# Squares' additions and low parts of weights on GpSimd at the end of the first layer

## The chip, the cores and the metric

The kernel runs on one core of a Trainium2 chip. The metric is the device time of one execution in microseconds (us), the median of three runs; lower is better. The core has five engines with queues of their own: PE (TensorE, matmuls), DVE (VectorE), ACT (ScalarE), POOL (GpSimd) and SP (SyncE, which here issues most weight loads). They run side by side and wait for each other by semaphores. Each works through its own list of instructions in a fixed order, so one instruction that waits holds up all that stand behind it on that engine.

## The reference, cut to what matters

A network of two layers over 1024 latent tokens and 256 context tokens, 1024 features wide. Layer 0 mixes tokens with a convolution module, layer 1 with attention (16 query heads, 4 key and value heads, all of 64 features). Each layer ends with a SwiGLU feed-forward network. Each part is normed before and after it:

```python
hx = rmsnorm(x, norm_g[i, 0]) * (1.0 + sc_x) + sh_x
yx = conv_module(hx, ...)             # layer 0; layer 1: attention_module
x = x + g_x * rmsnorm(yx, norm_g[i, 1])
fx = rmsnorm(x, norm_g[i, 2]) * (1.0 + scf_x) + shf_x
x = x + gf_x * rmsnorm(swiglu(fx, ffn_w1[i], ffn_w3[i], ffn_w2[i]), norm_g[i, 3])
```

```python
def attention_module(hx, hc, wq, wk, wv, wo, q_g, k_g, cos, sin, need_ctx):
    qx = apply_rope(rmsnorm((hx @ wq).reshape(B, S, N_HEADS, HEAD_DIM), q_g), cos, sin)
    kx = apply_rope(rmsnorm((hx @ wk).reshape(B, S, N_KV_HEADS, HEAD_DIM), k_g), cos, sin)
    vx = (hx @ wv).reshape(B, S, N_KV_HEADS, HEAD_DIM)
    ...
```

`rmsnorm` needs the sum over all features of the squares of a token's values.

## The kernel before

Features lie on the 128 partitions, tokens along the free axis; a tile of 1024 features is eight pieces of 128 features, k or d from 0 to 7. The tokens are the context, the left 512 and the right 512 latent tokens (below "left" and "right").

A float32 product is made of three faster ones. Each operand is split into a high part, rounded, and a low part, what is left; high times high, low times high and high times low are added in one PSUM bank. For a weight piece `wload` does the split: SP loads the raw piece (L143), ACT casts it to the high part (`wh`, L144), and a subtraction makes the low part (`wl`): L148 on DVE or L150 on POOL. The counter `share` chooses between them: it grows by `lo_dve` with every piece, and at 1 the subtraction goes to DVE. `lo_dve` is 1 for nearly all of the kernel before, so that all subtractions are on DVE. There are three buffers for raw pieces here (`wr` twice, `q` once), and three each for the high and low parts.

The end of the first layer is a place where three things overlap:

- The feed-forward network of the right tokens ends. Its last product is evicted from PSUM, d by d, by an addition on DVE (`evict`, L926), and behind each eviction `sq_acc` squares the piece on ACT (L390, into one of four buffers `sb`) and adds the square to the row sums `acc` (L391). PE then sums over the partitions (L365).
- The left tokens, finished earlier, are normed for the attention: `apply`, for each k, multiplies (DVE, L399, into one of the same four `sb`), makes the high part (ACT, L404) and the low part (DVE, L405) of the input to the attention.
- The projections of the left tokens start: keys (PE L183 to L185, in two banks for the even and odd features), values (L172 to L174 with the weight as the first operand, 256 columns), and the eight pieces of the query weights (L172 to L174).

Then the norm of the right tokens' output is applied (`final`: L693 and L696 on DVE, results stored by POOL's L1374), its squares are added (L391 again), and the right tokens are projected in the same way. `qk_pair` norms and rotates keys and queries: squares on ACT (L1007, L1008), sums on PE (L1015), products with cosine and sine on DVE (L1033 to L1036), the split (ACT L1040, DVE L1042). POOL issues the loads of cosine and sine (L1052, L1053), the stores of keys and queries (L1056, L1080) and the loads of what was stored (L1095, L1102). The first matmul of the attention is L1116, and `attention` sets `lo_dve` to 1 itself.

The order on each engine is not written out. Pieces of work are generators (`pump` runs the background queue `bgq` next to the main one by estimated times), and a scheduler below them orders the instructions of each engine by its own estimates of their durations. A change of engine therefore also reorders others.

Of the kernel before, what the change touches and what calls it, by code (L numbers as in the profile page):

```python
# [12 lines left out]
ALU = mybir.AluOpType  # L13
# [42 lines left out]
class Kern:  # L56
# [323 lines left out]
                                    self.c["ident"][:w, :w])  # L380
        return pb[:, :n]

    def sq_acc(self, acc, src, k):
        nc = self.nc
        n = src.shape[-1]
        if k == 0:
            nc.scalar.activation(acc, src, AF.Square)
            return
        sq = self.sb(n)
        nc.scalar.activation(sq, src, AF.Square)  # L390
        nc.vector.tensor_tensor(acc, acc, sq, op=ALU.add)  # L391

    def apply(self, src, pb, l, i, segs, hi, lo, k, full=None):

# [404 lines left out]
    def ffn(self, l, fs, ytags, htags, boxes, tanh=False, parts=1, tail=None, fast=None):  # L799
# [3 lines left out]
        nc = self.nc  # L803
# [142 lines left out]
        def last(ds, j, c0, c1, ws, sums):  # L946

            fts = GROUPS[-1]
            G = len(fts)
            outs = [self.bank("mm") for _ in ds]  # L950
            self.mm3s(outs, [lambda k, d=d: ws[d * G + k] for d in ds],
                      lambda k: [v[:, c0:c1] for v in slot[fts[k]][j]], G, c1 - c0)
            for d, out in zip(ds, outs):
                evict(len(GROUPS) - 1, out, j, d, c0, c1, sums)
# [15 lines left out]
        for j, n in enumerate(ns):  # L970
            for part in range(parts):
                c0, c1 = part * n // parts, (part + 1) * n // parts
                if tail is None:
                    yacc = yaccs[j] if len(ns) > 1 else self.acc(n)
                    sums = lambda yd, d: self.sq_acc(yacc, yd, d)
                else:
                    sums = tail[part]

                m = 4 if parts > 1 and part == 0 else 2 if j == 0 and part == 0 else 1
                d = 0  # L980
                while d < KT:
                    last(range(d, d + m), j, c0, c1, ws, sums)
                    yield 3 * G * m * (c1 - c0) / 2400
                    d += m
                    m = 1
                if tail is None:
                    boxes[j].append((ys[j], yacc))
                else:
                    boxes[j].append(ys[j][:, :, c0:c1])
# [201 lines left out]
    def build(self):  # L1191
        nc, a, c = self.nc, self.a, None
# [216 lines left out]
        self.drain()  # L1409
        self.root = True  # L1410
        hs = self.T("HS", [P, 4, 512])
        self.bgq.append(self.qkv(hL[0], CTX, 512, self.wk, hs[:, :2], (hs[:, 2:],)))
        self.pump(7)
        self.kub = self.T("KB", [P, 2 * TOK], F32R)
# [309 lines left out]
```

## Time and profile before

| | |
|---|---|
| median of 3 runs | 2939.29 us (2937.05 to 2940.01) |
| the profiled execution | 2938.98 us, of which the span from the first to the last instruction is 2937.2 us |
| granted PE clock, mean | 0.987 |
| busy share of the span | PE 97%, DVE 74%, ACT 45%, POOL 8% |
| key projection of the left tokens on PE | 1440.98 to 1463.34 us |
| first matmul of the attention | 1573 us |

The profile is of one execution. Times of rows count from the start of the span. A row of a timeline has the start, the duration, the engine, the line, the operation and its operands by the program's names, and in brackets the idle time of the engine before it and what ended that. Where a row stands for several instructions in a row (x2), the duration is that of all. A row of the windows has, behind the stretch and its length, the busy time and count of PE, the weight loads, DVE, ACT and POOL, then the granted PE clock, the share of the DMA engines and GB/s.

### The profile page before, as it was taken

How to read it: one execution, taken by the hardware profiler on the slowest of the kernel's cores; microseconds unless marked ns; L12 is line 12 of the kernel's file. 1: busy time of each engine (PE TensorE's matmuls, PEld its weight loads, DVE VectorE, ACT ScalarE, POOL GpSimd, SP SyncE). 2: the span in 40 equal slices, each digit the busy share in tenths (PEclk: the TensorE clock that was granted, in tenths of full speed). 3: DMA queues.
4: the chain of work that ended last, by engine and by line, in shares of the span. 5: the costliest groups of instructions: out<-in, count | busy, mean ns of one | idle time of the engine just before them, and what ended most of it. 6: DMA issues, size and time to landing. Idle time of an engine off the chain costs nothing.

```text
span 2937.2 us, 42731 instructions
## 1 busy us (share of the span) xinstructions
PE 2847.7 (97%) x16462; PEld 2446.1 (83%) x16462; DVE 2160.7 (74%) x3746; ACT 1335.5 (45%) x2229; POOL 222.6 (8%) x377
## 2 busy tenths in 40 slices
PE   7999989999999999999999999989999999999998
PEld 6888877888888889989888787767777778889997
DVE  6887788847556378877786899786666666786777
ACT  5222255532222245544445688645555543444444
POOL 0000001011022001000011111110000000010000
PEclk9999999999999999999999999999999999999999
DMA  6443444334356224333345211322222143353332
GB/s 249 140 120 98 116 131 145 135 116 143 115 175 198 65 74 165 114 104 112 109 156 170 88 46 46 97 87 81 66 73 83 60 149 99 110 170 104 102 98 75
DMA packets 131755, 336.58 MB, mean 115 GB/s; under 512 B 31328, under 2 KB 52864, under 8 KB 130656
## 3 DMA queue, kind: packets, MB, share of 16 engines
q1 hardware_dynamic: 78016, 222.33, 24.1%
q0 software_dynamic: 29344, 103.83, 10.7%
q10 hardware_dynamic: 24192, 7.70, 1.1%
q8 instruction: 129, 2.11, 0.3%
q14 instruction: 74, 0.61, 0.1%
HBM read 289.50 MB, written 38.93 MB: 112 GB/s over the span
## 4 chain that ended last, share of the span: by engine, by line
PE 86%; DVE 7%; ACT 2%; issue 2%; DMA 2%; ACTq 0%; POOL 0%; SPq 0%; DVEq 0%; POOLq 0%
PE ps L172 15%; PE ps L173 15%; PE ps L174 15%; PE ps L875 4%; PE ps L877 4%; PE ps L876 4%; PE ps L1116 4%; PE ps L1134 4%; PE ps L1140 2%; PE ps L454 2%; PE ps L455 2%; PE ps L456 2%; PE ps L1141 2%; PE ps L185 1%; PE ps L183 1%
## 5 line engine op out<-in xcount | busy, mean ns | idle before, releaser
L172 PE MATMUL ps<-T,wh 128*128 128x512 f32 (+1 forms) x1360 | 502.5, 370 | 1.4 <-ACT T L161 0.8
L174 PE MATMUL ps<-T,wl 128*128 128x512 f32 (+1 forms) x1360 | 500.4, 368 | 2.0 <-DVE wl L148 2.0
L173 PE MATMUL ps<-T,wh 128*128 128x512 f32 (+1 forms) x1312 | 481.4, 367 | 0.2 <-DVE T L164 0.2
L144 ACT CAST wh<-wr 128x1024 fp32r<-128x1024 f32 (+1 forms) x217 | 225.0, 1037 | 419.9 <-PE ps L173 307.2
L148 DVE TENSOR_TENSOR wl<-wr,wh 128x1024 fp32r<-128x1024 f32 (+1 forms) x217 | 261.9, 1207 | 168.5 <-ACT wh L144 167.1
L875 PE MATMUL ps<-T,wh 128*128 128x256 f32 x1092 | 310.7, 285 | 5.0 <-ACT wh L161 4.5
L876 PE MATMUL ps<-T,wh 128*128 128x256 f32 x1092 | 306.5, 281 | 0.0
L877 PE MATMUL ps<-T,wl 128*128 128x256 f32 x1092 | 305.4, 281 | 0.2 <-DVE wl L164 0.2
L1138 DVE TENSOR_TENSOR T<-ps,T 128x512 fp32r<-128x512 f32 x320 | 216.8, 687 | 107.6 <-ACT T L1137 106.8
L172 PEld LDWEIGHTS ps<-T,wh 128*128 128x128 f32 x1360 | 257.8, 190 | 43.7 <-ACT T L1506 1.7
L174 PEld LDWEIGHTS ps<-T,wl 128*128 128x128 f32 x1360 | 257.7, 190 | 42.4 <-DVE wl L148 2.2
L173 PEld LDWEIGHTS ps<-T,wh 128*128 128x128 f32 x1312 | 248.5, 189 | 38.2 <-DVE T L164 1.3
L1137 ACT CAST T<-ps 128x512 fp32r<-128x512 f32 x320 | 186.0, 586 | 191.1 <-PE ps L1134 177.6
L173 PE MATMUL ps<-HS,wh 128*128 128x512 f32 x656 | 257.9, 393 | 0.0
L172 PE MATMUL ps<-HS,wh 128*128 128x512 f32 x608 | 238.4, 392 | 0.9 <-ACT wh L144 0.9
L174 PE MATMUL ps<-HS,wl 128*128 128x512 f32 x608 | 237.5, 391 | 0.0
L875 PEld LDWEIGHTS ps<-T,wh 128*128 128x128 f32 x1092 | 206.1, 189 | 11.2 <-ACT wh L161 6.7
L876 PEld LDWEIGHTS ps<-T,wh 128*128 128x128 f32 x1092 | 206.6, 189 | 0.5
L877 PEld LDWEIGHTS ps<-T,wl 128*128 128x128 f32 x1092 | 206.2, 189 | 0.6 <-DVE wl L164 0.4
L1134 PE MATMUL ps<-cst,T 128*128 128x128 f32 x1100 | 189.6, 275 | 3.2 <-DVE T L1138 3.1
L1122 DVE TENSOR_SCALAR_CACHE_REDUCE T<-ps,rq 128x1280 f32<-128x1280 f32 x110 | 170.0, 1546 | 27.9 <-PE ps L1116 22.1
L1134 PEld LDWEIGHTS ps<-cst,T 128*128 128x128 f32 x1100 | 132.6, 141 | 49.5 <-DVE T L1138 30.8
(377 smaller groups left out, 6195.9 us busy)
## 6 DMA issues: line engine op xcount, KB each, us to landing
wr<-in_w SPq DMA_DIRECT2D x170, 512.0 KB, 3.6
wr<-in_pw SPq DMA_DIRECT2D x35, 512.0 KB, 3.5
HV<-in_wmodT POOLq DMA_DIRECT2D x56, 256.0 KB, 4.1
q<-in_wmodT POOLq DMA_DIRECT2D x56, 256.0 KB, 3.9
KB<-in_w SPq DMA_DIRECT2D x24, 512.0 KB, 3.6
HR<-in_w SPq DMA_DIRECT2D x23, 512.0 KB, 3.7
q<-in_w SPq DMA_DIRECT2D x23, 512.0 KB, 4.2
q<-qsd POOLq DMA_DIRECT2D x32, 256.0 KB, 3.3
```

Source lines behind the costliest of these rows:

```text
L144: nc.scalar.copy(hi, raw)
L148: nc.vector.tensor_tensor(lo, raw, hi.bitcast(F32), op=ALU.subtract)
L172: nc.tensor.matmul(out[:, :n], lhsT=wh, rhs=xh, start=k == 0, stop=False)
L173: nc.tensor.matmul(out[:, :n], lhsT=wh, rhs=xl, start=False, stop=False)
L174: nc.tensor.matmul(out[:, :n], lhsT=wl, rhs=xh, start=False, stop=k == nk - 1)
L875: nc.tensor.matmul(out, lhsT=wh, rhs=bh, start=first and k == 0, stop=False, **skip)
L876: nc.tensor.matmul(out, lhsT=wh, rhs=bl, start=False, stop=False, **skip)
L877: nc.tensor.matmul(out, lhsT=wl, rhs=bh, start=False, stop=k == 3, **skip)
L1122: nc.vector.tensor_scalar(out=pt, in0=sc, scalar1=rq[:, h:h + 1], scalar2=None, op0=ALU.mult, op1=ALU.min, accum_out=mn)
L1134: nc.tensor.transpose(tp[:, h * P:(h + 1) * P], Ps[h][:, j * P:(j + 1) * P], c["ident"])
L1137: nc.scalar.copy(ph, tp)
L1138: nc.vector.tensor_tensor(pl, tp, ph.bitcast(F32), op=ALU.subtract)
```

## The change

Two things move from DVE to POOL. In the feed-forward network of the right tokens in the first layer (`fast` is set there, and in the second layer's call too, where the sums are given from outside, so that nothing changes), the seven additions of squares go to POOL. And from the start of the left tokens' projections until the attention, `lo_dve` is 0, so that the subtractions of 18 weight pieces go to POOL: two of keys, two of values and eight of queries for the left tokens, two of keys, two of values and two of queries for the right ones.

```diff
-    def sq_acc(self, acc, src, k):
+    def sq_acc(self, acc, src, k, eng=None):
...
-        nc.vector.tensor_tensor(acc, acc, sq, op=ALU.add)
+        (eng or nc.vector).tensor_tensor(acc, acc, sq, op=ALU.add)
...
-                    sums = lambda yd, d: self.sq_acc(yacc, yd, d)
+                    sums = lambda yd, d: self.sq_acc(yacc, yd, d, nc.gpsimd if fast else None)
...
         hs = self.T("HS", [P, 4, 512])
+        self.lo_dve = 0.0
         self.bgq.append(self.qkv(hL[0], CTX, 512, self.wk, hs[:, :2], (hs[:, 2:],)))
```

What it moves shows in the order of each engine. PE from the last matmul of the right tokens' feed-forward network (`HS`) on, before the change (`T_12426` and `T_12427` are the high and low parts of the left tokens' normed input):

```order
L185 MATMUL ps<-HS,wl 128x512
L183 MATMUL ps<-T_12426,wh 128x512
L184 MATMUL ps<-T_12427,wh 128x512
L183 MATMUL ps<-T_12426,wh 128x512
L184 MATMUL ps<-T_12427,wh 128x512
L172 MATMUL ps<-wh,T_12426 128x256 x2
L365 MATMUL ps<-cst,acc 128x1 x4
L185 MATMUL ps<-T_12426,wl 128x512
```

And after it:

```order
L185 MATMUL ps<-HS,wl 128x512
L183 MATMUL ps<-T_12426,wh 128x512
L184 MATMUL ps<-T_12427,wh 128x512
L185 MATMUL ps<-T_12426,wl 128x512
L183 MATMUL ps<-T_12426,wh 128x512
L184 MATMUL ps<-T_12427,wh 128x512
L185 MATMUL ps<-T_12426,wl 128x512
```

Before, PE began the value projection and summed the right tokens' squares (L365) ahead of the key projection's third matmul of the first piece. Now the key projection's 48 matmuls stand in a row, and L365 behind the value projection.

POOL at the same place, after the change; before it L1052 follows the L685 directly, and then come the writes (L1056, L1374) with nothing between:

```order
L685 DMA T_12759<-x1d 128x2x512 x4
L150 ISA
L150 TENSOR_TENSOR wl<-q,wh 128x1024
L391 TENSOR_TENSOR acc<-acc,sb 128x512
L150 TENSOR_TENSOR wl<-wr_73,wh 128x1024
L391 TENSOR_TENSOR acc<-acc,sb 128x512 x4
L1052 DMA HS<-in_cos 128x512
L1053 DMA HS<-in_sin 128x512
L391 TENSOR_TENSOR acc<-acc,sb 128x512
L150 TENSOR_TENSOR wl<-wr_74,wh 128x1024
L391 TENSOR_TENSOR acc<-acc,sb 128x512
```

The additions and subtractions stand in one queue with the loads and stores that POOL issues. The ISA row is an instruction that loads code for the engine. Further on, the order after the change is:

```order
L1056 DMA ksd<-T_12538 128x2x512 x2
L150 TENSOR_TENSOR wl<-wr_74,wh 128x1024
L150 TENSOR_TENSOR wl<-q,wh 128x1024
L1095 DMA KB<-ksd 64x2x768 x2
L1374 DMA x2d<-T_8806 128x512 x8
L150 TENSOR_TENSOR wl<-wr_73,wh 128x1024
L150 TENSOR_TENSOR wl<-wr_74,wh 128x1024
L150 TENSOR_TENSOR wl<-q,wh 128x1024
```

Two low parts of query weights stand behind the stores of the keys (`ksd`), and three more low parts behind the stores of the right tokens' result (`x2d`). On DVE the seven L391 and the L148 leave, and the evictions L926 move ahead of the multiplications that they stood behind.

## The prediction

> **What bounds the kernel now.** I read the busy shares first, then the shares of the chain that ended last:
>
> ```profile
> PE 2847.7 (97%) x16462; PEld 2446.1 (83%) x16462; DVE 2160.7 (74%) x3746; ACT 1335.5 (45%) x2229; POOL 222.6 (8%) x377
> PE 86%; DVE 7%; ACT 2%; issue 2%; DMA 2%; ACTq 0%; POOL 0%; SPq 0%; DVEq 0%; POOLq 0%
> ```
>
> PE is the bound on the whole; DVE holds 7% of the chain. The change can only pay where PE waits for DVE, so next I read PE's timeline where the first layer ends (start, duration, line, names, and in brackets the idle time before it with its releaser), and beside it a window of the granted clock (the column after POOL):
>
> ```profile
> 1440.98 0.39 PE L183 MATMUL ps<-T,wh 128*128 128x512 f32 x1
> 1441.94 0.47 PE L183 MATMUL ps<-T,wh 128*128 128x512 f32 x1 [0.35 <-DVE T L926]
> 1444.46 0.35 PE L172 MATMUL ps<-wh,T 128*128 128x256 f32 x1 [1.82 <-DVE T L926]
> 1446.89 0.58 PE L172 MATMUL ps<-wh,T 128*128 128x256 f32 x1 [2.07 <-DVE T L926]
> 1448.81 1.87 PE L365 MATMUL ps<-cst,acc 128*128 128x1 f32 x8 [1.34 <-DVE acc L391]
> ...
> 1451.11 0.63 PE L183 MATMUL ps<-T,wh 128*128 128x512 f32 x1
> 1451.54 0.63 PE L184 MATMUL ps<-T,wh 128*128 128x512 f32 x1
> ...
> 1463.11 0.39 PE L185 MATMUL ps<-T,wl 128*128 128x512 f32 x1
> 1463.34 0.28 PE L173 MATMUL ps<-wl,T 128*128 128x256 f32 x1
> ```
>
> ```profile
> 1451.00:1456.00 5.00, 5.00 (x13) 3.84 (x13) 1.82 (x2) 0.00 (x0) 0.00 (x0) 0.50 0.92 328
> ```
>
> The reader is to see two losses. PE stands idle 0.35 + 1.82 + 2.07 + 1.34 = 5.58 us, always for DVE; and from 1451 to 1456 the clock is half, so that the matmuls start 0.43 us apart (1451.11, 1451.54) where the last one of the stage takes 0.23 (1463.11 to 1463.34). DVE in that stretch:
>
> ```profile
> 1438.53 0.74 DVE L399 SCALAR_TENSOR_TENSOR sb<-T,col,ps 128x512 f32<-128x512 f32 x1
> ...
> 1441.11 0.68 DVE L926 TENSOR_TENSOR T<-ps,T 128x512 f32<-128x512 f32 x1
> ...
> 1443.63 0.68 DVE L926 TENSOR_TENSOR T<-ps,T 128x512 f32<-128x512 f32 x1
> ...
> 1446.15 0.68 DVE L926 TENSOR_TENSOR T<-ps,T 128x512 f32<-128x512 f32 x1
> ...
> 1448.08 0.68 DVE L391 TENSOR_TENSOR acc<-acc,sb 128x512 f32<-128x512 f32 x1
> 1448.68 1.22 DVE L148 TENSOR_TENSOR wl<-q,wh 128x1024 fp32r<-128x1024 f32 x1
> 1449.81 0.74 DVE L405 SCALAR_TENSOR_TENSOR T<-sb,mod,T 128x512 fp32r<-128x512 f32 x1
> ```
>
> DVE runs without a gap, and each PE wait ends as an L926 eviction ends (1441.79, 1444.31, 1446.83) or the last L391 (1448.76). PE waits for PSUM banks and for the row sums, not for the key projection's input: tile k of it (L405) needs to be there only at 1440.98 + 1.37 k (six matmuls of 0.2275 a tile), the last at 1450.5, and here it ends at 1450.55.
>
> **The change, term by term.** Moved to POOL: 7 additions of 128x512 (0.68 each on DVE) and 18 subtractions of 128x1024 (1.22 each on DVE).
>
> *Price on POOL.* No POOL tensor_tensor is in the trace. The nearest rows, and the two engines' queues ahead of the place:
>
> ```profile
> L1147 POOL COPY sb<-sums x32: 394/402/1365, 1605.4 to 2363.0; 128x256 f32<-128x256 f32 x32
> q14 instruction: 74, 0.61, 0.1%
> 1422.04 2.89 POOL L685 DMA_DIRECT2D T<-x1d  x4 [163.99 <-PE ps L877]
> 1441.44 0.57 POOL L1052 DMA_DIRECT2D HS<-in_cos  x1 [16.51 <-PE ps L185]
> 1429.43 1.05 ACT L144 CAST wh<-q 128x1024 fp32r<-128x1024 f32 x1
> 1435.55 1.06 ACT L144 CAST wh<-wr 128x1024 fp32r<-128x1024 f32 x1 [1.75 <-PE ps L184]
> ```
>
> A copy of 256 columns takes 0.402 us, so 1.6 for 1024 columns and 0.8 for 512 if a second input is free, 3.2 and 1.6 if it counts like the first. I take the middle, 2.4 and 1.2. The Trainium skill (GPSIMD Engine Reference, 3.1 Elementwise) measures an fp32 tensor_tensor of 2048 columns at 4497 ns; an estimate by that page is 2.25 and 1.1, which no run here shows yet and which would leave the sum where it is.
>
> *Library.* The new order has one instruction on POOL that the old lacks, an ISA row ahead of the first subtraction: it loads code. Nothing shows its cost: from nothing (the first L1147 takes no longer than the others) to 47 us (0.1% of 16 engines' span, if all of the instruction queue q14's time stood in one line). I take the low end, since the L1147 row is nearer. Cover: POOL is idle from 1424.9, and the first low part can start only at 1430.48, when its cast ends: 5.5 us free. The first addition is wanted by the L399 that stood at 1438.53, which takes over its buffer, and with 2.4 + 1.2 ahead of that a load of up to some 10 us (1424.9 + 10 + 3.6 = 1438.5) costs nothing; beyond it each us delays L399, L405 and so PE. The Trainium skill (GPSIMD Engine Reference, 2.1 Instruction dispatch) puts the first call of a freshly loaded kernel at 5.95 us; by it the sum is unchanged as well, and no run here shows it.
>
> *PE's stop goes.* The new order has PE run the key projection's 48 matmuls in a row. They take 48 x 0.2275 = 10.92 us, where the stage took 22.36 (1440.98 to 1463.34). In these 22.36 stood also two V matmuls (0.24) and L365, which now stands behind V (0.79, row below). Net: 22.36 - 10.92 - 1.03 = **-10.4 us**, 5.6 of it idle time and 4.8 slow clock. POOL by the middle prices: first subtraction done 1432.9, second (cast ready 1436.6) 1439.0, additions 2 to 5 by 1443.8, cos and sin issued (0.57 each) by 1444.9, addition 6 at 1446.1, third subtraction 1448.5, addition 7 at 1449.7. Each is before PE's need: the third's is the V projection at 1451.9. If this cover fails, it is L399 (its buffers now come free by POOL) and then L405 that is late.
>
> *The port.* Here a row counts against the change. POOL's 32 copies take 0.40, but for one:
>
> ```profile
> 2133.81 1.22 DVE L148 TENSOR_TENSOR wl<-wr,wh 128x1024 fp32r<-128x1024 f32 x1
> 2134.95 0.68 DVE L1138 TENSOR_TENSOR T<-ps,T 128x512 fp32r<-128x512 f32 x1
> 2133.91 1.36 POOL L1147 COPY sb<-sums 128x256 f32<-128x256 f32 x1
> ```
>
> The copy starts 0.1 us behind a DVE subtraction of two SBUF tiles, and ends 0.32 after DVE has left that for an instruction with one input in PSUM: it stood still meanwhile. The other direction, DVE standing behind POOL, no row shows. The Trainium skill (SBUF — State Buffer, Who interferes with whom) says that a DVE instruction with two SBUF inputs shares a read port with GpSimd, and that whoever issues first blocks the other fully; the trace agrees with it in this one row, for POOL as the blocked one. If POOL holds DVE up in the same way, L405 (sb and T) must take turns with POOL. From 1436.6: a subtraction 2.4, additions 2 to 6 6.0, two issues 1.1, a subtraction 2.4, six L405 4.4: 16.3 us, so the last tile at 1452.9 instead of 1450.5, +2.4, and more where PE waits for a tile between. Bounds: 0 (POOL only stands back), and with POOL at 3.2 and 1.6 another 0.8 x 2 + 0.4 x 5 = 3.6, so +6. I take **+3**.
>
> *The right half's norm.* Behind it DVE works in one block for the right half, and PE follows:
>
> ```profile
> 1478.30 1.40 DVE L693 SCALAR_TENSOR_TENSOR T<-T,col,ps 128x512 f32<-128x512 f32 x2
> ...
> 1488.98 1.22 DVE L148 TENSOR_TENSOR wl<-q,wh 128x1024 fp32r<-128x1024 f32 x1
> ...
> 1496.61 1.22 DVE L148 TENSOR_TENSOR wl<-wr,wh 128x1024 fp32r<-128x1024 f32 x1
> 1497.74 0.69 DVE L391 TENSOR_TENSOR acc<-acc,sb 128x512 f32<-128x512 f32 x1
> ...
> 1503.28 0.15 DVE L341 SCALAR_TENSOR_TENSOR nr<-nq,nr 128x4 f32<-128x4 f32 x1
> ```
>
> The chain of waits names PE's steps there, and PE's timeline the start of the right half's keys:
>
> ```profile
> 1477.14 0.44 PE ps L379 x4
> ...
> 1499.37 0.79 PE ps L365 x8
> ...
> 1501.04 0.43 PE ps L174
> ...
> 1503.60 0.43 PE ps L174
> ```
>
> ```profile
> 1509.20 0.71 PE L183 MATMUL ps<-T,wh 128*128 128x512 f32 x2
> ```
>
> The key projection ends at 1463.34 - 10.4 + 3 - 1.0 = 1454.9 (the 1.0 is the work that now stands behind V); V takes as long as before (1463.34 to the broadcast at 1477.14, 13.8), so 1468.7; L365 0.8; from a norm's L365 to its last small operation (1500.16 to 1503.43) 3.3, less the L148 of 1.13 that stood in it, 2.2; the broadcast and L693 at 1472.5, against 1478.3: -5.8. L693 to the last L391 took 20.1 us (1478.30 to 1498.43) with two L148 in it; they leave, and POOL puts two of 2.4 beside two-input instructions: at half a collision each 20.1 - 2.3 + 2.4. So the last L391 is 5.7 earlier. Then two more subtractions leave DVE, and a slow stretch (eight matmuls at 0.43 for 0.23 from 1501.04 to 1503.60, 1.6 us) may close with the wait ahead of it: -1.3. The right half's K starts 7 us earlier. With no collisions it would be 12, with POOL at its upper price about 0.
>
> *The rest.* The other eight subtractions lie beside PE-bound projections. They stand in POOL's queue behind writes that wait:
>
> ```profile
> L1374 POOL DMA_DIRECT2D x2d<-T x8 | 4.4, 551 | 3.8 <-DVE T L696 2.7 <-DMA KB<-ksd 1.1
> L1056 POOL DMA_DIRECT2D ksd<-T x4 | 2.9, 729 | 38.9 <-ACT T L1040 37.5 <-DVE T L1042 1.3
> ```
>
> Behind L1056 wait two low parts of the query weights, behind L1374 three; and behind the low parts wait the raw buffers, so SP's weight loads. By the order the writes are ready a few us before those low parts are needed; 0, bounds -1 to +4. From the first attention on everything is in order behind PE, so an advance is kept.
>
> Sum: the stop -10.4, the port +3, the norm's chain +0.4 (the advance of 7.4 arrives at the right half's K as 7.0), the rest 0: **-7.0**. The profiled execution took 2938.98 (span 2937.2 and 1.8 around it), 0.3 under the median of the runs: **2932.0**.
>
> **Rivals.** A measurement tells 0.2%, 5.9 us, from no change.
> 1. POOL blocks nobody but itself, as in the one row: -12, 2927. For it: only that direction is seen. Against: one row is little.
> 2. Collisions eat all: POOL at 3.2 and 1.6, each collision whole, +6 and +5 on -10.4: 2938 to 2940. For it: L405, L391, L696 and L1033 to L1042 are nearly all of DVE's work here, and have two SBUF inputs. The Trainium skill's rule of the port (SBUF — State Buffer, Who interferes with whom), taken in both directions, would have this rival at POOL's upper price; no run here shows the second direction yet.
> 3. Slower: the library load is long. PE stops for each us above 10; at 21 us the gain is gone, at 30 it is 9 lost, 2948. For it: an unseen price; against: POOL's first copy is no slower than its later ones. The same sign comes if POOL's queue, with low parts behind writes behind DVE, holds SP's loads up for over 10 us: it decides where V's or Q's low part lands after PE has reached it.
> 4. PE's stop only moves: were DVE not what PE waits for, nothing would change. Against: all four brackets name it.
>
> **How the numbers follow.** Forecast (-3 to -10) 0.36; rival 1 0.28; rivals 2 and 4 0.18; rival 3 0.18. Faster by over 0.2%: rival 1 and two thirds of the forecast, 0.52; within: the third, and most of rivals 2 and 4, 0.27; slower 0.21. The range goes from 2924 (rival 1, a cheaper POOL) to 2944 (rival 2 and a start of 3); outside are most of 3 and a little below. The forecast's own is 2929 to 2936.
>
> **What would show it.** Right: PE without brackets from 1441 to 1452 and a clock of 1.0 there; L365 behind V; L150 at 1.6 to 3.2 us on POOL; L693 at about 1472; the right half's K at about 1502. Collisions: L405 or L391 longer than 0.74 or 0.69 beside an L150. Wrong: POOL's first L150 later than 1440, or PE waiting for wl of L150 in the V or query projections.

## The result, and the profile after

The changed kernel takes 2954.38 us (median of 6 runs, 2951.62 to 2962.18), the kernel before 2939.65 (6 runs, 2937.05 to 2942.14): ratio 1.0051, 95% interval 1.0042 to 1.0061. It is slower by 14.7 us where 7 us faster was forecast, and outside the range of 2924 to 2944. The profiled execution's span is 2950.2 us, 13.0 more than before. The first matmul of the attention starts at 1585.4 instead of 1573.4, so 12.0 of the 13.0 are lost before the attention.

The page's busy shares and shares of the chain, changed kernel:

```profile
PE 2853.7 (97%) x16462; PEld 2451.2 (83%) x16462; DVE 2168.0 (73%) x3721; ACT 1334.3 (45%) x2229; POOL 277.0 (9%) x402
PE 86%; DVE 8%; issue 2%; ACT 2%; DMA 1%; POOL 1%; ACTq 0%; SPq 0%; DVEq 0%; POOLq 0%
```

DVE has 25 instructions fewer and yet is busy 7.3 us longer. Its busy time holds standing time: that is the first sign. PE's timeline, and two windows of the key projection with the granted clock behind the POOL column:

```profile
1453.29 0.80 PE L184 MATMUL ps<-T,wh 128*128 128x512 f32 x1 [4.46 <-DVE T L405]
...
1470.49 0.66 PE L1030 MATMUL ps<-cst,sm 128*128 128x128 f32 x4 [1.55 <-DVE sm L1026]
1475.05 0.95 PE L365 MATMUL ps<-cst,acc 128*128 128x1 f32 x8
1481.80 1.11 PE L379 MATMUL ps<-cst,nr 128*128 128x128 f32 x4 [3.40 <-DVE nr L341]
...
1509.35 1.86 PE L365 MATMUL ps<-cst,acc 128*128 128x1 f32 x8 [3.80 <-DVE acc L391]
...
1518.46 1.22 PE L183 MATMUL ps<-T,wh 128*128 128x512 f32 x2 [2.06 <-ACT T L404]
...
1535.10 0.39 PE L173 MATMUL ps<-wl,T 128*128 128x256 f32 x1 [1.11 <-POOL wl L150]
```

```profile
1441.00:1446.00 5.00, 5.00 (x24) 4.14 (x23) 3.82 (x6) 3.30 (x5) 4.76 (x4) 1.00 0.30 105
...
1451.00:1456.00 5.00, 2.71 (x6) 2.17 (x7) 4.21 (x4) 0.72 (x1) 2.76 (x4) 0.51 0.37 105
```

The old stops are gone: PE runs without a gap and at full clock from 1441. Then it stands 4.46 us for one L405, and the half clock is back behind that. Of the waits shown, four name DVE (4.46, 1.55, 3.40 and 3.80 us), one ACT (2.06), and only one a low part from POOL (1.11). All of PE's brackets from 1441 to the attention add up to 9.5 us before and 19.3 us now, 9.9 us more of PE standing idle, most of the 12.0. The same places on DVE and on POOL:

```profile
1438.37 2.35 DVE L405 SCALAR_TENSOR_TENSOR T<-sb,mod,T 128x512 fp32r<-128x512 f32 x1
...
1448.11 5.79 DVE L405 SCALAR_TENSOR_TENSOR T<-sb,mod,T 128x512 fp32r<-128x512 f32 x2 [0.56 <-ACT T L404]
...
1476.24 4.50 DVE L337 TENSOR_SCALAR nh<-nv 128x4 f32<-128x4 f32 x1
...
1494.72 5.09 DVE L1033 TENSOR_TENSOR HS<-T,HS 128x1024 f32<-128x1024 f32 x1 [0.99 <-ACT T L1010]
...
1502.68 2.88 DVE L391 TENSOR_TENSOR acc<-acc,sb 128x512 f32<-128x512 f32 x1
```

```profile
1437.77 2.39 POOL L150 TENSOR_TENSOR wl<-wr,wh 128x1024 fp32r<-128x1024 f32 x1 [2.90 <-ACT wh L144]
1440.14 6.66 POOL L391 TENSOR_TENSOR acc<-acc,sb 128x512 f32<-128x512 f32 x4
...
1447.87 1.30 POOL L391 TENSOR_TENSOR acc<-acc,sb 128x512 f32<-128x512 f32 x1
1449.12 2.34 POOL L150 TENSOR_TENSOR wl<-wr,wh 128x1024 fp32r<-128x1024 f32 x1
1451.42 1.25 POOL L391 TENSOR_TENSOR acc<-acc,sb 128x512 f32<-128x512 f32 x1
...
1476.01 2.41 POOL L150 TENSOR_TENSOR wl<-wr,wh 128x1024 fp32r<-128x1024 f32 x1
1478.37 2.34 POOL L150 TENSOR_TENSOR wl<-q,wh 128x1024 fp32r<-128x1024 f32 x1
...
1493.98 4.74 POOL L150 TENSOR_TENSOR wl<-wr,wh 128x1024 fp32r<-128x1024 f32 x2
...
1532.68 2.37 POOL L150 TENSOR_TENSOR wl<-wr,wh 128x1024 fp32r<-128x1024 f32 x1 [19.08 <-ACT wh L144]
```

Two L405 that took 1.41 before take 5.79 and end 1.2 us after POOL's run of three ends (1452.67). L337, four columns wide, takes 4.50 instead of 0.17 and ends with POOL's two subtractions (1480.7). L1033 takes 5.09 instead of 1.22, again over two of them (to 1498.72). In these three places DVE stands behind a whole run of POOL. At 1438.37 it does not: that L405 ends 0.6 us after the L150 beside it, and POOL's next addition is the longer for it (1.75 us for 1.3). Taking each DVE instruction between 1427 and 1590 against the median of the same kind in the profile before, 15 took over 0.1 us longer, 30 us of standing in all. That sum is not the loss: standing costs time only where PE waits for what DVE is to make.

### The profile page after: what moved, and what is told of

It reads as the page before. It is cut to its first block, busy times and chain, and to the rows that moved or that the text cites. A ratio compares the mean times of both kernels' runs of the same rounds, so it can differ in the third digit from the quotient of the medians.

```text
span 2950.2 us, 42741 instructions
## 1 busy us (share of the span) xinstructions
PE 2853.7 (97%) x16462; PEld 2451.2 (83%) x16462; DVE 2168.0 (73%) x3721; ACT 1334.3 (45%) x2229; POOL 277.0 (9%) x402
## 4 chain that ended last, share of the span: by engine, by line
PE 86%; DVE 8%; issue 2%; ACT 2%; DMA 1%; POOL 1%; ACTq 0%; SPq 0%; DVEq 0%; POOLq 0%
PE ps L172 15%; PE ps L173 15%; PE ps L174 14%; PE ps L875 4%; PE ps L877 4%; PE ps L876 4%; PE ps L1116 4%; PE ps L1134 4%; PE ps L1140 2%; PE ps L454 2%; PE ps L456 2%; PE ps L455 2%; PE ps L1141 2%; PE ps L184 1%; PE ps L185 1%
## 5 line engine op out<-in xcount | busy, mean ns | idle before, releaser
L148 DVE TENSOR_TENSOR wl<-wr,wh 128x1024 fp32r<-128x1024 f32 (+1 forms) x205 | 247.4, 1207 | 168.9 <-ACT wh L144 167.5
```

Of the source, the lines that this page charges most:

```text
L148: nc.vector.tensor_tensor(lo, raw, hi.bitcast(F32), op=ALU.subtract)
```

## The experiments

Times are medians; "before" is the kernel before on the same chip, 2940.4 to 2941.0 in the three sets. The theory is the port: a POOL instruction that reads SBUF holds DVE up (said below as: DVE stands; its row counts the time as busy). Its rivals are late results and a longer queue on POOL, and the new order of PE.

**The port by itself.** Behind the last result of the kernel before, sections are added in which both engines start together:

```diff
+        sec(None, d_tt)              # DVE: 8 subtractions 128x512, two SBUF inputs
+        sec(p_tt(1024, 3), None)     # POOL: 3 additions 128x1024
+        sec(p_tt(1024, 3), d_tt)
+        sec(p_tt(1024, 3), d_ps)     # DVE: one input in PSUM
+        sec(p_tt(1024, 3), d_ts)     # DVE: 8 tensor_scalar 128x4
+        sec(p_tt(1024, 3), d_cp)     # DVE: 8 copies 128x512
+        sec(p_set(4), d_tt)          # POOL: 4 memset 128x1024
+        sec(p_tt(512, 6), d_tt)
+        sec(p_tt(256, 12), d_tt)
+        sec(p_ind, d_tt)             # POOL: 3 additions 128x1024, each into another tile
+        sec(p_ind, d_ts)
```

> The kernel before, with eleven sections of POOL and DVE instructions added behind its last result; both engines start each section together. Theory (a POOL instruction that reads SBUF keeps DVE's two-input instructions out for as long as POOL runs): eight DVE additions of two SBUF tiles take 4.9 us alone, and end only after POOL's three of 1024 columns (7.2 us) beside them; a chain of POOL instructions lets one DVE instruction in between two at best; with one input in PSUM, or beside POOL's memset, which reads nothing, they take 4.9 again. Small tensor_scalar and copy instructions of DVE, with one input, wait too, since 128x4 ones stood for 4.5 us in the changed kernel. Rival (POOL's results come late, DVE itself isn't slowed): DVE takes 4.9 us in every section.

DVE's rows in the order of these sections (the second has none), then six of POOL's; each row is a whole section:

```profile
2939.45 5.78 DVE L1668 TENSOR_TENSOR T<-T 128x512 f32<-128x512 f32 x8 [5.62 <-ACT T L1645]
2953.93 11.92 DVE L1668 TENSOR_TENSOR T<-T 128x512 f32<-128x512 f32 x8 [8.70 <-ACT T L1645]
2966.69 5.77 DVE L1672 TENSOR_TENSOR T<-ps,T 128x512 f32<-128x512 f32 x8 [0.84 <-ACT T L1645]
2974.78 7.74 DVE L1676 TENSOR_SCALAR T<-T 128x4 f32<-128x4 f32 x8 [2.32 <-ACT T L1645]
2983.56 12.73 DVE L1680 COPY T<-T 128x512 f32<-128x512 f32 x8 [1.04 <-ACT T L1645]
2997.13 5.78 DVE L1668 TENSOR_TENSOR T<-T 128x512 f32<-128x512 f32 x8 [0.84 <-ACT T L1645]
3003.75 11.51 DVE L1668 TENSOR_TENSOR T<-T 128x512 f32<-128x512 f32 x8 [0.84 <-ACT T L1645]
3016.09 8.59 DVE L1668 TENSOR_TENSOR T<-T 128x512 f32<-128x512 f32 x8 [0.84 <-ACT T L1645]
3029.46 10.58 DVE L1668 TENSOR_TENSOR T<-T 128x512 f32<-128x512 f32 x8 [4.77 <-ACT T L1645]
3040.93 6.48 DVE L1676 TENSOR_SCALAR T<-T 128x4 f32<-128x4 f32 x8 [0.90 <-ACT T L1645]
```

```profile
2945.92 7.17 POOL L1653 TENSOR_TENSOR T<-T 128x1024 f32<-128x1024 f32 x3 [304.37 <-ACT T L1644]
2953.84 7.83 POOL L1653 TENSOR_TENSOR T<-T 128x1024 f32<-128x1024 f32 x3 [0.75 <-ACT T L1644]
...
2991.10 4.45 POOL L1663 MEMSET T<- 128x1024 f32 x4 [0.34 <-ACT T L1643]
...
3016.30 12.18 POOL L1653 TENSOR_TENSOR T<-T 128x256 f32<-128x256 f32 x12 [3.04 <-ACT T L1645]
3029.37 6.49 POOL L1658 TENSOR_TENSOR T<-T 128x1024 f32<-128x1024 f32 x3 [0.90 <-ACT T L1644]
3040.78 5.59 POOL L1658 TENSOR_TENSOR T<-T 128x1024 f32<-128x1024 f32 x3 [4.92 <-ACT T L1644]
```

Alone the eight take 5.78 us (4.9 was expected), and 11.92 beside POOL: 6.1 of POOL's 7.8 us are added, while POOL loses 0.7, about one DVE instruction. With one input in PSUM nothing is added (5.77). Eight tensor_scalar of four columns need 7.74, as long as POOL runs, though each takes 0.17 in the kernel; the copies, whose time alone was not measured, 12.73. The memset section (5.78) says nothing: POOL's row, which reads nothing and so waited for nothing, ends at 2995.55, before DVE's row starts at 2997.13. It ran beside the copies instead, and they end after it (2996.29). With pieces of 256 columns DVE loses only 2.8 us, and POOL takes 12.18.

The last two sections try what the changed kernel has, POOL instructions that do not work on each other's result. DVE's eight take 10.58, so 4.8 of POOL's 6.49 us are added; the eight small ones 6.48. DVE does not stand over the whole run here: of all 48 two-input instructions none took over 2.80 us, so none stood behind more than one POOL instruction. The probe shows the collision, and not why DVE missed its turns in the changed kernel.

**The parts alone.** First the squares on POOL and all low parts on DVE; then the low parts on POOL and the squares on DVE:

```diff
-        self.lo_dve = 0.0
```

> Only the seven additions of squares are on POOL; all low parts stay on DVE. Theory (port): POOL reads for 7 x 1.3 = 9 us only, all beside L405, and nothing later: within 4 us of before, 2936 to 2943. Rival (POOL's queue: low parts behind writes, raw buffers held): no low part is on POOL, so the advance of the prediction comes through, 2930 or less.

```diff
-                    sums = lambda yd, d: self.sq_acc(yacc, yd, d, nc.gpsimd if fast else None)
+                    sums = lambda yd, d: self.sq_acc(yacc, yd, d)
```

> Only the 18 low parts are on POOL; the squares are added on DVE. Theory (port): nearly all of the 12 us come back, since the long stands (L337 4.5, L1033 5.1, L391 2.9, L1034 4.2 us) are behind low parts: 2948 to 2955. Rival (the squares' additions, late by POOL's price, and L365 behind the value projection, make the loss): 2938 to 2944.

The squares alone: 2933.39, ratio 0.9976 (0.9967 to 0.9986), 7.6 us faster, between what the two theories said. DVE stands only 2.0 us in sum there. The low parts alone: 2954.33, ratio 1.0043 (1.0028 to 1.0058), as slow as both together, with 28 us of standing. So the loss comes with the low parts.

**The order alone.** No work on POOL; the first two low parts get a better rank among DVE's instructions, and PE's key projection then stands in a row but for its last six matmuls, which are among the value projection's (`self.first` is set to 2 where the left tokens' projections begin):

```diff
-            nc.vector.tensor_tensor(lo, raw, hi.bitcast(F32), op=ALU.subtract)
+            self.first -= 1; off = -100 if self.first >= 0 else 0; self.tc.cur_priority += off; nc.vector.tensor_tensor(lo, raw, hi.bitcast(F32), op=ALU.subtract); self.tc.cur_priority -= off
```

> No work on POOL: all as before, but the first two low parts (keys) get a better rank in the scheduler, and so PE's key projection stands in a row, as in the changed kernel. If PE's stop of 5.6 us and its slow clock come from the order of PE and DVE alone, this gives the prediction's first term without the port: 8 to 10 us faster, 2929 to 2932. If the stop was DVE's lack of time, it comes back elsewhere, within 3 us of before.

2931.24 (2929.37 to 2934.35), ratio 0.9968 (0.9954 to 0.9982), 9.8 us faster. PE and its clock in this kernel:

```profile
1441.00:1446.00 5.00, 5.00 (x24) 4.13 (x22) 4.84 (x9) 2.94 (x5) 0.22 (x1) 1.00 0.28 105
1446.00:1451.00 5.00, 5.00 (x31) 4.45 (x30) 4.21 (x7) 1.36 (x2) 0.60 (x2) 1.00 0.17 35
```

DVE does all that it did, and PE doesn't stop there. The stop was a matter of order, not of too much work on DVE.

**Reads against writes, in place.** DVE does all the work as before; POOL does something unused in each raw buffer behind it. In one kernel it subtracts, which reads two SBUF tiles, in the other it writes zeros twice (each line stands behind the subtraction of L148):

```diff
+            self.beside and nc.gpsimd.tensor_tensor(raw, raw, hi.bitcast(F32), op=ALU.subtract)
```

> As before, DVE makes all low parts and adds all squares; beside it POOL subtracts once more in the raw buffer of each of the 18 weight pieces (two SBUF inputs, 2.4 us each), and nobody uses what it writes. Theory (port): the loss of the low parts alone comes back without any result of POOL being waited for: 10 to 20 us slower than before, 2950 to 2960, with DVE instructions of two inputs and small ones standing up to 5 us. Rival (results of POOL come late, POOL's own queue): nothing waits for a low part from POOL; 2939 to 2943, but for what POOL's writes of keys and queries lose.

```diff
+            self.beside and [nc.gpsimd.memset(raw, 0.0) for _ in range(2)]
```

> As the kernel with POOL's unused subtractions, but POOL writes each of the 18 raw buffers twice with zeros (1.1 us each) and reads nothing: the same hold on the raw buffers, on POOL's queue and on SP's loads, without a read of SBUF. Theory (port): within 3 us of before, 2938 to 2944. Rival (raw buffers held longer, POOL's queue longer): as slow as with the subtractions, 2950 to 2960.

With reads 2961.3, ratio 1.0069 (1.0053 to 1.0084): 21 us slower, with no result of POOL in use. With writes 2943.83, ratio 1.0012 (1.0002 to 1.0021): 3.4 us. Raw buffers and POOL's queue are held in both, but the difference of 17.5 us is not reading alone, because the two kernels differ in order too: with writes DVE's order stays near that of the kernel before, with reads the scheduler moved much of it. DVE stands 14 us in sum beside the reads, and POOL stands as well. Yet the longest waits of PE, 5.9 and 6.4 us, are for DVE's own low parts, and these were late by their place in DVE's order: the cast for the first was ready at 1479.78, and DVE came to it at 1492.04, behind the right tokens' norm. In the kernel before, the L148 of that piece (its row comes first below) stood ahead of the norm. How much of the 17.5 us is reading and how much the order was not parted. From the kernel that reads then two waits of PE, the cast, and places on DVE and POOL; last, two places in the kernel that writes:

```profile
1476.83 1.22 DVE L148 TENSOR_TENSOR wl<-wr,wh 128x1024 fp32r<-128x1024 f32 x1
```

```profile
1493.31 0.80 PE L174 MATMUL ps<-T,wl 128*128 128x512 f32 x1 [5.92 <-DVE wl L148]
...
1529.60 0.79 PE L185 MATMUL ps<-T,wl 128*128 128x512 f32 x1 [6.38 <-DVE wl L148]
...
1478.73 1.05 ACT L144 CAST wh<-wr 128x1024 fp32r<-128x1024 f32 x1
...
1492.04 1.21 DVE L148 TENSOR_TENSOR wl<-wr,wh 128x1024 fp32r<-128x1024 f32 x1
...
1496.65 6.22 DVE L391 TENSOR_TENSOR acc<-acc,sb 128x512 f32<-128x512 f32 x3
...
1493.40 6.18 POOL L148 TENSOR_TENSOR wr<-wr,wh 128x1024 f32<-128x1024 f32 x1 [1.04 <-DVE wl L148]
1499.55 2.78 POOL L148 TENSOR_TENSOR q<-q,wh 128x1024 f32<-128x1024 f32 x1
```

```profile
1504.54 4.53 DVE L1022 TENSOR_SCALAR rq<-nr 128x16 f32<-128x16 f32 x1
...
1508.07 0.97 POOL L148 MEMSET q<- 128x1024 f32 x1
...
1532.47 3.40 DVE L1026 COPY sm<-nr 128x512 f32<-128x512 f32 x1
```

POOL's subtraction at 1493.40 takes 6.18 for 2.4 while DVE runs one two-input instruction behind the other. And with writes DVE stands too: one small tensor_scalar until the run of memsets ends (1509.04), 4.4 us, and one copy 3.0 us, while the two-input subtractions beside memsets stay at 1.2. So POOL need not read to hold DVE up; which instructions collide depends on the kind of DVE instruction.

**Shorter pieces.** The changed kernel, each low part in four pieces:

```diff
-            nc.gpsimd.tensor_tensor(lo, raw, hi.bitcast(F32), op=ALU.subtract)
+            [nc.gpsimd.tensor_tensor(lo[:, i:i + 256], raw[:, i:i + 256], hi[:, i:i + 256].bitcast(F32), op=ALU.subtract) for i in range(0, n, 256)]
```

> The changed kernel with each low part made by POOL in four pieces of 256 columns. Theory (port, held through a run of POOL instructions): DVE gets in between some pieces where POOL waits for its own result, but independent pieces run on and each costs 0.6 to 1 us, so POOL's total grows: 2948 to 2958, no better than the changed kernel by more than 5 us. Rival (only long instructions block): the stands fall to under 1 us each and most of the 13 us come back: 2940 or less.

2943.76, ratio 1.0008 (0.9999 to 1.0017): 10.6 us of the 14.7 come back, against the theory as it was put. DVE's longest stand is 2.0 us, though its stands still add up to some 18 us, and in one place POOL gives way. Its row, then DVE's where the two begin:

```profile
1483.91 12.96 POOL L150 TENSOR_TENSOR wl<-wr,wh 128x256 fp32r<-128x256 f32 x8
```

```profile
1483.59 1.21 DVE L1033 TENSOR_TENSOR HS<-T,HS 128x1024 f32<-128x1024 f32 x1
```

Eight pieces, 0.74 each where undisturbed, take 12.96 beside the chain of the right tokens, and the first of them alone 6.22. It is not their length that made POOL wait: the unused subtraction of 1024 columns, above, took 6.18 for 2.4. In both places DVE was at work when POOL's instruction came (1483.59 against 1483.91 here) and kept on, one instruction behind the other; in the changed kernel POOL's L150 had begun (1493.98) when DVE's L1033 came (1494.72), and there DVE stood. Shorter pieces did make each stand shorter. PE then waits for low parts (1.07 and 1.45 us), and longer for ACT (2.61, 3.70 and 4.27 us).

**Which low parts.** Only the first three on POOL with the squares; then only the two of keys, with the squares on DVE:

```diff
+        self.first = 3        # low parts on POOL, then DVE again
```

> The changed kernel with only its first three low parts on POOL (two of keys, one of values) and the squares; the other 15 are on DVE again. Theory (port): the one stand of 4.4 us at the end of the key projection may stay, all later ones (some 22 us in sum) go, and with them PE's waits of 1.5, 3.4 and 3.8 us: 2930 to 2938. Rival (the harm is done in the key projection, by the squares and the first low parts): 2945 or more.

> As before, but the two low parts of the left tokens' key weights are on POOL (POOL reads for 2 x 2.4 us, apart from each other). Theory (port): two stands of at most 2.4 us, and PE's key projection stands in a row: 2929 to 2936. Rival (any low part on POOL costs more than it frees on DVE): 2939 or more.

With three and the squares 2941.18, ratio 1.0 (0.999 to 1.0009); the 4.4 us stand of L405 is there and no later one. So the other 15 low parts cost 13 to 14 us. It missed its expected range all the same. Its right half's K still starts 4.1 us earlier than before, but its attention 1.5 us later (1574.9 against 1573.4); where the stretch between loses that was not settled. With the two of keys only: 2937.82, ratio 0.9986 (0.9977 to 0.9995), a small gain of 2.7, less than expected.

**Two attempts at more.** The squares on POOL together with the better rank; and the better rank for all 18 low parts, all on DVE (`self.first = 18`):

> No low part on POOL; the seven additions of squares on POOL and the better rank of the first two low parts on DVE together. Each alone gained 8 to 10 us. Theory (both gain by taking away the same stop of PE): no more than the better of the two, 2929 to 2933. Rival (they add up): 2922 to 2926.

> No work on POOL; all 18 low parts get the better rank on DVE, not only the first two. If low parts that come late are what else PE waits for before the attention (0.6 us at the query weights), 1 to 3 us better than with two: 2927 to 2930. If DVE's chain of the right tokens is what PE waits for there, low parts ahead of it push it back: 2932 to 2938.

Together 2936.39, ratio 0.9986 (0.9977 to 0.9994), worse than either alone, which neither theory said. All 18: 2934.53, ratio 0.9978 (0.9968 to 0.9987), also behind two. L365 shows a part of why; its row with only the rank, and with both:

```profile
1453.41 0.95 PE L365 MATMUL ps<-cst,acc 128*128 128x1 f32 x8
```

```profile
1467.64 0.95 PE L365 MATMUL ps<-cst,acc 128*128 128x1 f32 x8
```

| kernel | time | L365 | first L693 | right half's K |
|---|---|---|---|---|
| before | 2940.5 | 1448.8 | 1478.3 | 1509.2 |
| rank of two low parts | 2931.2 | 1453.4 | 1470.5 | 1499.5 |
| squares on POOL | 2933.4 | 1447.7 | 1470.0 | 1500.9 |
| rank of all 18 | 2934.5 | 1456.7 | 1473.0 | 1503.8 |
| squares and rank | 2936.4 | 1467.6 | 1472.8 | 1502.9 |
| two of keys on POOL | 2937.8 | 1469.4 | 1474.8 | 1505.4 |
| three on POOL and squares | 2941.2 | 1469.8 | 1474.9 | 1505.1 |
| low parts on POOL | 2954.3 | 1470.9 | 1478.3 | 1513.0 |
| changed | 2954.4 | 1475.1 | 1483.0 | 1518.5 |

In the three kernels with L365 at 1467.6 to 1469.8, where the scheduler puts it behind the value projection, the right tokens' norm starts 2 to 4 us later than with the rank of two. The rest between "squares and rank" and "rank of two" comes behind the right half's K (the attention starts at 1572.8 against 1565.2); what it is made of was not settled.

## Why the prediction was wrong

- *PE's stop, -10.4.* Right: the order of PE was read rightly, PE ran in a row from 1441.64 until the L405 stood, and the order alone gave 9.8 us.
- *The price on POOL, 2.4 and 1.2.* Right: 2.4 for a subtraction (median of the undisturbed and disturbed ones) and 1.25 to 1.3 for an addition at the places shown.
- *The library, nothing.* Right: whatever it took lay within POOL's idle 5.6 us. The first subtraction starts as its cast ends and takes no longer than others:

```profile
1431.23 2.40 POOL L150 TENSOR_TENSOR wl<-q,wh 128x1024 fp32r<-128x1024 f32 x1 [5.58 <-ACT wh L144]
```

- *The port, +3.* This step failed, by its size and by its reach. The mechanism was there, but the sum let L405 and POOL take turns. POOL's next instruction went ahead of the waiting DVE one: of two L405 the first stood 4.4 us over a run of three. One did take its turn (1438.37); why these did not is open. The key projection ended at 1459.4, where 10.92 us in a row from 1441.64 would have been 1452.6: 6.9 us, with the slow clock that followed the stand, where the term had 3 and its bound 6.
- *The norm's chain, +0.4.* This step failed by more. It counted half a collision for two subtractions, and only for instructions with two wide inputs. In fact small ones stood as well: L337 4.3 us, between L365 and L379, where 2.2 us had been set down for the whole chain, which took 5.8 (1476.00 to 1481.80). L693 started at 1482.96, not 1472.5 (the prediction's own terms add up to 1472.8). From it to the last L391 it took 26.3 us (to 1509.29), not 20.2. The right half's K started at 1518.5, not 1502.
- *The rest, 0 with +4 at most.* From that K to the first L1116 it was 66.9 us instead of 64.2, so +2.7: inside the bounds. The queue behind the writes shows in none of PE's waits there. 1.1 us is the wait for one low part: POOL, idle for 19 us before it, began as the cast ended and took 2.37 us where DVE takes 1.22. L1033, L1034 and L337 stood there too; how much of the other 1.6 us is theirs was not measured.
- *The rivals.* Rival 2 named the right mechanism and gave it 0.18 with others, and by its worst case only the loss of the gain. It summed the wide collisions and left the small ones and the runs out. Rival 3 had the right sign, but neither of its reasons: the library cost nothing, and the one wait for a low part from POOL, 1.1 us, was not for its queue.

The whole: the order's gain of 10 us came, and PE's waits behind DVE's stands took more than that, so that 12 us were lost before the attention. That POOL's reads hold DVE's two-input instructions up is shown by the probe, with both inputs in SBUF against one in PSUM; that the low parts and not the squares make the loss, by the parts alone; that DVE's stands reach PE, by the brackets that name L405, L341 and L391. The unused subtractions agree with it, but their order differs as well.

## What to carry to other kernels

If POOL is idle and DVE is short, ask first whether DVE lacks time or its order is bad: here a better rank for two instructions gave 9.8 us with no engine changed. Work on POOL that reads SBUF is not beside DVE's two-input and small instructions but largely in their place, at POOL's price of 2.4 us for what takes DVE 1.2. If it has to go there, keep it away from DVE's chains for which PE waits; cutting it into pieces of 256 columns gave 10.6 us back here.

## What the runs showed of the hardware

- In three places of the changed kernel a run of POOL instructions with SBUF inputs held DVE for what was left of the run (4.4 us over three, 4.3 and 3.9 over two); in the probe never for more than one POOL instruction (at most 2.80 us for one of 0.69). What decides is open. Not only DVE instructions with two SBUF inputs were held: tensor_scalar on four columns stood 4.3 us, a four-column copy (L373) 2.0. With an input in PSUM nothing was held (5.77 against 5.78 us). The Trainium skill (SBUF — State Buffer, Who interferes with whom) has copies and tensor_scalar, in some modes, and two-input instructions contend with GpSimd; the runs agree, but by its rule of who issues first a waiting DVE instruction should not have been passed by POOL's next one.
- POOL stood in the same way where DVE was at work first and kept on: a subtraction of 1024 columns took 6.18 us for 2.4, a piece of 256 columns 6.22 for 0.74.
- A small tensor_scalar stood 4.4 us and a copy of 512 columns 3.0 us beside runs of POOL's memsets, which read nothing.
